# Summing the later modulations of a diffusion layer over partitions by block transposes and one 0/1 matrix, with fewer of their steps in the context's loop

## The chip, the core and the metric

The kernel runs on one core of a Trainium2 chip. Its time is the device time of one execution in microseconds, of which the median of several runs counts. The engines are named as in the profile: PE is TensorE's matmul side and PEld its weight loads, DVE is VectorE, ACT is ScalarE, POOL is GpSimd, SP is the engine whose queue issues nearly all transfers here.

## What is computed

One layer of a diffusion backbone over 1024 latent tokens and 256 context tokens of 1024 channels, all in float32: a gated feed-forward half step, a mixer (short convolution beside grouped-query attention), and a second half step. Each of the three parts is normalised and modulated by a shift, a scale and a gate, which are rows of one vector per stream (latent `l`, context `c`):

```python
mod_lat = (jax.nn.silu(c) @ w_mod[layer] + b_mod[layer])[:, None, :]
mod_ctx = (jax.nn.silu(c_ctx) @ w_mod[layer] + b_mod[layer])[None, None, :]
ml = jnp.split(mod_lat, N_MOD, axis=-1)          # nine rows of 1024
x = x + 0.5 * ml[2] * swiglu(modulate(rms_norm(x, norm1_g[layer]), ml[0], ml[1]), ...)
...
x = x + 0.5 * ml[8] * swiglu(modulate(rms_norm(x, norm3_g[layer]), ml[6], ml[7]), ...)
```

`w_mod` is 1024 by 9216. The latent stream needs all nine rows of it, the context stream the first five. In the kernel a modulation row is a table with the channel on the partition: channel 128j + p stands in column j of partition p.

## The kernel before, in words

**Products.** The large products run on PE as three fp32r matmuls of 128x128 by 128x512 each (high by high, high by low, low by high), and by a Winograd scheme, so that one "product" is 12 matmuls. Weights arrive by a load on SP's queue into a tile `raw`; POOL adds and subtracts them into tiles `s` where the scheme needs it; ACT casts them to fp32r and DVE subtracts the cast, which gives a pair called `wl` in the traces (`split`, L189). Four such pairs can wait ahead of PE (`W_BUFS`), five PSUM banks `ps` take products, two banks `pt` take short results and transposes, one bank `po` is left.

**Stages.** After a head (tokens are loaded, turned and normalised, the first modulations are made by another way, `column_mod` and `second_mod`) comes the first half step, L1337: a loop over 22 columns j of the hidden layer. For each j PE does five products (`second`, `third`), DVE and ACT finish the hidden columns, and SP stores them (`hd`). At j = 11 a second loop runs inside, the **context's loop** (L1347): for i = 0 to 11 the context's 256 tokens are multiplied with the weights of the columns already done, in matmuls of 256 columns (`h1ch`, `h1cl`), and every second i their hidden columns go through the second weight (`hidc`, `wo`, sums in `cacc`). From j = 12 on the context's products run along with the latent ones (`side`, L1262). Then come the half step's output (`row_products`, L1429), the mixer's products with the convolution (L1445 on), queries and keys, the attention, the merge, the second half step (its loop over 22 columns at L2158) and the last norm.

**Later modulations.** All modulation rows that are not needed in the head are made by the generator `later_mod` (L266), in halves of 512 channels. For each half it loads eight tiles `rawm` of `w_mod` (128x512, 256 KB each), and DVE adds each, times a column of silu(c), into an accumulator `macc` of 128x512 per stream. So 128 partial sums stand on the partitions for each of 512 channels. Then, per stream: ACT and DVE split `macc` into two fp32r tiles (`acch`, `accl`), PE multiplies a column of ones (`ones_r`, 128x1) with each (two matmuls with an output of 1x512 in a bank `pt`), ACT copies that row out (`mrow`), four small transfers on SP's queue lay the row out on 128 partitions (`mcol`), and DVE adds the bias into `modl` or `modc`. In all 22 streams are summed: one each for the context's second halves of rows 1 and 0, twelve for rows 2 to 4, two for row 5, four for rows 6 and 7, two for row 8.

**Who calls it.** The generator is advanced step by step: `run(steps, n)` takes n steps. In the first half step the number per j is `STEPS` (L43), and in the context's loop 3 per i (L1353). The steps of rows 1, 0, the context's norm (`normc`, which makes `h1ch` and `h1cl`) and rows 2 to 5 lie in `steps`; rows 6 and 7 are taken during the mixer's products (L1457, L1460), row 8 in the second half step (L2160).

**What sets the order.** Every instruction is recorded in the program's order and then placed by a scheduler, which works with a time line of its own and puts instructions of an engine where it expects them to be ready. The engines then run their lists strictly in order. Instructions recorded as pinned (`matmul(..., pinned=True)`, L132) keep the program's order among each other. Short tiles of 128x512 (`rawm`, `macc`, `s`, `u`, `c`, `v`, `b`, `nt` and others) share one pool of 11 buffers (L102, `ttile`), so that a tile of one kind can wait for the release of another kind.

**The norm of the second half step.** `norm1` of the class `Winograd` (L526) takes the sum of squares over channels, which lies on the partitions in two accumulators `sq_acc` and `sq`, and sums it by eight matmuls with `ones` as the moving operand (`rstd_cols`, L245), which puts token 128j + p on partition p of column j; an inverse root follows on DVE (`rs_a`, `rs_t`, `rs_y`), which is then spread by PE (`bcast`). The mixer's object is made with `plain=True`, that of the second half step is not; the first half step has its root from elsewhere.

Of the kernel before, what the change touches and what calls it, by code (L numbers as in the profile page):

```python
# [9 lines left out]
F32 = mybir.dt.float32  # L10
F32R = mybir.dt.float32r
I32 = mybir.dt.int32
AF = mybir.ActivationFunctionType
ALU = mybir.AluOpType
AX = mybir.AxisListType
# [3 lines left out]
P = 128  # L19
D = 1024  # L20
# [8 lines left out]
EPS = 1e-6  # L29
# [10 lines left out]
AHEAD = 3  # L40
FILLS = (24,) + 4 * (11,) + 11 * (10,)
SIDE_FROM = 12
STEPS = (0, 4, 4, 4, 4, 5, 5, 5, 5, 5, 5, 4, 11)  # L43
WAIT = 4
AH1, HALVES, WH = 12, 8, (4, 5, 6, 7, 12, 13, 14, 15, 20, 21, 22, 23)
RESIDENT, AH2, AH3 = 2, 9, 12
# [5 lines left out]
def tile_dit_layer(  # L52
# [63 lines left out]
    def ttile(name, n=512, dt=F32):  # L116
        t = tpool.tile([P, 512], dt, tag="t", name=uniq(name))
        return t[:, :n]

    def small(name, n, dt=F32):  # L120
        return spool.tile([P, n], dt, tag=f"s{n}_{name}", name=uniq(name))
# [4 lines left out]
    def ps_t(n=512):  # L126
        return psum.tile([P, 512], F32, tag="t", name=uniq("pt"), bufs=2)[:, :n]
# [4 lines left out]
    def matmul(out, w, x, start, stop, pinned=False, on=False):  # L132

        inst = pe.matmul(out, w, x, start=start, stop=stop, skip_group_check=on)
        if pinned or in_order[0]:
            tc.keep_in_program_order(inst)
# [14 lines left out]
    make_identity(nc, ident[:])  # L151
    ones = const.tile([P, 1], F32, name="ones")
    dve.memset(ones[:], 1.0)
    ones_r = const.tile([P, 1], F32R, name="ones_r")
    act.copy(out=ones_r[:], in_=ones[:])


    cols = const.tile([P, P], F32, name="cols")
# [30 lines left out]
    def split(src, hi, lo, lo_eng=None, hi_eng=None):  # L189

        if hi_eng is dve:
            dve.tensor_copy(out=hi, in_=src)
        else:
            act.copy(out=hi, in_=src)
        (lo_eng or dve).tensor_sub(out=lo, in0=src, in1=hi.bitcast(F32))
# [43 lines left out]
    def rsqrt_cols(a, n):  # L239

        y = small("rs_y", n)
        rsqrt_into(y[:], small("rs_t", n)[:], a)
        return y

    def rstd_cols(accs, n, dim):  # L245
# [10 lines left out]
        dve.tensor_scalar(out=a[:], in0=pss, scalar1=dim * EPS, scalar2=None, op0=ALU.add)  # L256
        return rsqrt_cols(a[:], nt)

    def bcast(y, n):

        pr = ps_t(n)
        for j in range(n // P):
            transpose(pr[:, j * P : (j + 1) * P], y[:, j : j + 1].to_broadcast([P, P]), pinned=True)
        return pr

    def later_mod(m, halves=(0, 1), streams=None):  # L266

        if streams is None:
            streams = (0, 1) if m < 5 else (0,)
        for half in halves:  # L270
            accs = [ttile(f"macc{v}") for v in streams]
            o = m * D + half * 512
            for k in range(KD):
                raw = ttile("rawm")
                load(out=raw, in_=w_mod[0, k * P : (k + 1) * P, o : o + 512])
                for acc, v in zip(accs, streams):
                    s = silu_c[:, v * 8 + k : v * 8 + k + 1]
                    if k == 0:
                        dve.tensor_scalar(out=acc, in0=raw, scalar1=s, scalar2=None, op0=ALU.mult)
                    else:  # L280
                        dve.scalar_tensor_tensor(out=acc, in0=raw, scalar=s, in1=acc, op0=ALU.mult, op1=ALU.add)
                yield
            for _ in range(WAIT):
                yield
            for acc, v in zip(accs, streams):
                ah, al = ttile("acch", dt=F32R), ttile("accl", dt=F32R)
                split(acc, ah, al)
                for _ in range(3):
                    yield
                mod, pm = (modl, modc)[v], ps_t()  # L290
                matmul(pm[:1], ones_r[:], ah, start=True, stop=False, pinned=True)
                matmul(pm[:1], ones_r[:], al, start=False, stop=True, pinned=True)
                row = ttile("mrow")
                act.copy(out=row[:1], in_=pm[:1])
                mcol = small("mcol", 4)
                for j in range(4):
                    sp.dma_start(out=mcol[:, j : j + 1], in_=row[:1, j * P : (j + 1) * P])
                c0 = m * 8 + half * 4
                dve.tensor_add(out=mod[:, c0 : c0 + 4], in0=mcol[:], in1=bcol[:, c0 : c0 + 4])
            yield  # L300

    def summed_mod(m, half, acc):
# [139 lines left out]
    def run(steps, n=None):  # L442

        if n is None:
            for _ in steps:
                pass
        else:
            for _ in range(n):
                next(steps, None)
# [13 lines left out]
    class Winograd:  # L463
# [60 lines left out]
            self.n_squares[ch] = n + 1  # L524

        def norm1(self):  # L526
            y = self.rstd1 or rstd_cols(self.accs[C1], 512, D)
            yield
            pr = bcast(y, 512)
            yield  # L530
            late = {3: [], 4: [], 7: []}
            for k in range(4):
                f, h, t34 = self.h0[k], atile("h12", (P, 2, 512)), atile("t34", (P, 2, 512))
                b12, b22, t3, t4 = h[:, 0], h[:, 1], t34[:, 0], t34[:, 1]
                for i, b in ((k, b12), (k + 4, b22)):
                    dve.tensor_mul(out=b, in0=self.xs(i, C1), in1=pr)
                    self.shifted(b, i)
                t1, t2 = ttile("nt"), ttile("nt")
                dve.tensor_sub(out=t1, in0=b12, in1=f[:, 0])
                dve.tensor_sub(out=t2, in0=b22, in1=t1)  # L540
                dve.tensor_sub(out=t4, in0=t2, in1=f[:, 1])
                self.keep(6, k, t2)
                dve.tensor_sub(out=t3, in0=b22, in1=b12)
                self.keep(5, k, t1)
                for i, t in ((3, b22), (4, t4), (7, t3)):
                    late[i].append(t)
                yield
            for i in (7, 4, 3):
                for k, t in enumerate(late[i]):
                    self.keep(i, k, t)  # L550
                yield
# [785 lines left out]
    for j in range(NH):  # L1337
        half1.side = side(j) if j >= SIDE_FROM else None
        if j > SIDE_FROM and j % 2:
            raws = context_rows(j)  # L1340
        u, c = half1.next_first()
        v, b = half1.second(u)
        spill(c, b, j, C0)
        spill(*half1.third(u, v), j, C1)
        run(steps, STEPS[min(j, len(STEPS) - 1)])
        if j == SIDE_FROM - 1:
            for i in range(SIDE_FROM):  # L1347
                if i % 2 == 0:
                    raws = context_rows(i + 1)
                do = side(i, ps_s)  # L1350
                for step in (1, 2, 0, 4):
                    do(step, half1.left())
                run(steps, 3)  # L1353
                if i % 2 == 0:
                    context_last()
                    ws = context_parts(i + 1, raws)
                else:
                    pending.append((i, ws))
        elif j > SIDE_FROM and j % 2:
            pending.append((j, context_parts(j, raws)))  # L1360
        elif j >= SIDE_FROM:
            context_last()
# [875 lines left out]
```

## Time and profile before

| | |
|---|---|
| median of 3 runs | 2657.49 us (2656.51 to 2659.11) |
| the profiled execution | 2662.96 us, of which its span is 2661.2 us |
| PE busy | 2609.7 us (98%), 13337 matmuls |
| DVE busy | 2054.2 us (77%) |
| ACT busy | 1229.3 us (46%) |
| POOL busy | 549.2 us (21%) |
| share of PE in the chain that ended last | 82% |

The share of the busy time tells which engine is full, not where it waits. Matmuls overlap, so that one of 391 ns in the table of groups costs PE less: what one costs is the distance from its start to the next one's. A time line's row gives start and duration, the operation, the tiles as out<-in, the shape of the stationary operand (rows*columns), the output's shape, the number of merged instructions, and in brackets the engine's idle time before it with what ended that. A row of windows gives, for each engine, busy time and number of instructions in that stretch, then the granted clock of PE (1.00 is full) and the share of the 16 DMA engines.

### The profile page before, as it was taken

The page shows a single profiled execution, that of the slowest core. Times are in us where ns is not written, and L with a number is a line of the kernel's source. Part 1 is how long each engine was busy: PE and PEld are TensorE (multiplying, and loading weights), DVE is VectorE, ACT ScalarE, POOL GpSimd, SP SyncE. Part 2 cuts the span into 40 slices and gives each one's busy share as a digit, 9 for nine tenths or more (in the row PEclk, how much of TensorE's full clock was granted, in tenths as well). Part 3 has the DMA queues.
Part 4 walks back from the last instruction along what each step waited for, and adds up shares of the span by engine and source line. Part 5 has one row for each costly group of instructions (what it writes and reads, how often), then busy time and mean ns, then how long its engine had stood idle before and what let it go on. Part 6 is the DMA issues. An engine that isn't in the chain of part 4 may idle for free.

```text
span 2661.2 us, 37166 instructions
## 1 busy us (share of the span) xinstructions
PE 2609.7 (98%) x13337; PEld 2197.8 (83%) x13337; DVE 2054.2 (77%) x3366; ACT 1229.3 (46%) x2434; POOL 549.2 (21%) x374
## 2 busy tenths in 40 slices
PE   8999999999999999999999999999999999999998
PEld 5788998888788878888898788788887888888888
DVE  5988887786887898887687766676888777666885
ACT  5633443333454643333366666666437333334444
POOL 1243011221010044332310011111030334320110
PEclk9999999999999999999999999999999999999999
DMA  8656753345984355443536321122443654327841
GB/s 269 223 183 192 230 171 119 112 127 195 314 187 108 106 170 171 132 141 113 172 123 207 103 64 64 60 68 64 133 126 123 202 179 135 98 76 258 224 100 68
DMA packets 386128, 393.14 MB, mean 148 GB/s; under 512 B 29326, under 2 KB 268056, under 8 KB 385944
## 3 DMA queue, kind: packets, MB, share of 16 engines
q1 hardware_dynamic: 376920, 373.48, 43.8%
q0 software_dynamic: 9024, 17.30, 4.0%
q8 instruction: 104, 1.70, 0.3%
q14 instruction: 80, 0.66, 0.1%
HBM read 313.07 MB, written 77.59 MB: 147 GB/s over the span
## 4 chain that ended last, share of the span: by engine, by line
PE 82%; DVE 8%; DMA 4%; ACT 3%; issue 2%; SPq 1%; POOL 1%; DVEq 0%; ACTq 0%; POOLq 0%
PE ps L90 67%; PE po L90 7%; PE pt L90 7%; DVE wl L90 1%; ACT pl L90 1%; DVE pts L90 1%; DVE u L90 1%; DMA rawm<-in_w_mod_dram 1%; DMA o<-qd 1%; DMA hid<-hd 1%; SPq L90 1%; DVE r L90 1%; DMA y<-yd 1%; DVE v L90 1%; DVE m L90 1%
## 5 line engine op out<-in xcount | busy, mean ns | idle before, releaser
L90 PE MATMUL ps<-r,wl 128*128 128x512 f32 x5496 | 1272.7, 391 | 14.2 <-DVE wl L90 6.2
L90 PEld LDWEIGHTS ps<-r,wl 128*128 128x128 f32 x5496 | 1030.4, 189 | 234.3 <-DVE wl L90 8.7
L90 ACT CAST wl<-s 128x512 fp32r<-128x512 f32 x266 | 164.2, 619 | 339.6 <-PE ps L90 254.3
L90 ACT CAST wl<-raw 128x512 fp32r<-128x512 f32 x298 | 184.0, 620 | 230.8 <-PE ps L90 124.7
L90 DVE TENSOR_TENSOR wl<-raw,wl 128x512 fp32r<-128x512 f32 x296 | 213.9, 728 | 74.9 <-ACT wl L90 74.0
L90 POOL TENSOR_TENSOR s<-raw 128x512 f32<-128x512 f32 x68 | 98.9, 1454 | 819.2 <-DMA raw<-in_ffn_w_in_dram 369.9
L90 DVE TENSOR_TENSOR wl<-s,wl 128x512 fp32r<-128x512 f32 x266 | 235.4, 886 | 32.6 <-ACT wl L90 31.1
L90 POOL TENSOR_TENSOR s<-raw,s 128x512 f32<-128x512 f32 x68 | 103.6, 1524 | 363.5 <-DVE wl L90 354.4
L90 DVE SCALAR_TENSOR_TENSOR macc<-rawm,silu_c,macc 128x512 f32<-128x512 f32 x168 | 147.9, 893 | 11.8 <-DMA rawm<-in_w_mod_dram 11.2
L90 DVE TENSOR_REDUCE m<-ps 128x1 f32<-128x512 f32 (+1 forms) x192 | 110.8, 595 | 59.4 <-PE ps L90 59.4
L90 DVE TENSOR_TENSOR u<-u,ps 128x512 f32<-128x512 f32 x183 | 124.1, 678 | 27.2 <-PE ps L90 26.8
L90 ACT CAST pts<-pt 128x512 fp32r<-128x512 f32 x160 | 93.8, 587 | 102.3 <-PE pt L90 102.2
L90 PE MATMUL ps<-tw,r 128*128 128x256 f32 x1008 | 126.6, 287 | 5.7 <-DVE tw L90 5.3
L90 PEld LDWEIGHTS ps<-tw,r 128*128 128x128 f32 x1008 | 123.7, 194 | 6.6 <-DVE tw L90 5.9
L90 DVE TENSOR_TENSOR pts<-pt,pts 128x512 fp32r<-128x512 f32 x160 | 109.4, 685 | 24.1 <-ACT pts L90 21.7
L90 PE MATMUL ps<-rh,wl 128*128 128x512 f32 x360 | 122.2, 390 | 0.0
L90 ACT CAST rh<-hid 128x512 fp32r<-128x512 f32 x132 | 80.8, 619 | 85.1 <-PE ps L90 76.6
L90 PE MATMUL po<-pts,v 128*128 128x512 f32 x384 | 120.1, 422 | 0.0
L90 ACT ACTIVATE pl<-ps,nm,qscale 128x512 f32<-128x512 f32 x128 | 98.6, 775 | 42.8 <-DVE nm L90 42.7
L90 POOL TENSOR_TENSOR s<-raw,raw 128x512 f32<-128x512 f32 x74 | 112.0, 1513 | 9.6 <-DVE macc L90 3.3
L90 PE MATMUL ps<-kl,qs 128*128 128x512 f32 x384 | 110.2, 395 | 2.5 <-ACT pl L90 2.2
L90 PE MATMUL ps<-y,wc 128*128 128x512 f32 x384 | 105.5, 395 | 1.9 <-DVE g L90 1.9
(361 smaller groups left out, 4648.1 us busy)
## 6 DMA issues: line engine op xcount, KB each, us to landing
raw<-in_ffn_w_in_dram SPq DMA_DIRECT2D x128, 512.0 KB
raw<-in_ffn_w_out_dram SPq DMA_DIRECT2D x72, 512.0 KB
rawm<-in_w_mod_dram SPq DMA_DIRECT2D x128, 256.0 KB
raw<-in_w_in_dram SPq DMA_DIRECT2D x53, 512.0 KB
hid<-hd SPq DMA_DIRECT2D x40, 512.0 KB
ws<-in_ffn_w_out_dram POOLq DMA_DIRECT2D x30, 512.0 KB, 6.3
ucd<-uc SPq DMA_DIRECT2D x26, 512.0 KB
hd<-c SPq DMA_DIRECT2D x39, 256.0 KB
```

What stands on the lines that cost most here:

```text
L90: inst = getattr(self.engine, name)(*args, **kw)
```

## The change

`later_mod` sums over partitions in another way. For each stream DVE transposes `macc` in blocks of 32x32 (`mturn`), so that a block's 32 partial sums of one channel lie in one row, and adds them up with one reduction over 32 neighbours; 16 numbers per partition are left, which are written over the start of the first accumulator. One float32 matmul per half, with the 0/1 matrix `same4` as the stationary operand (128x128, a one wherever row and column agree modulo 32), adds the four groups of 32 partitions and leaves the result on all four of them. DVE then takes from each group of 32 partitions the columns that belong to it: four additions of 32x4 per stream, which read PSUM and add the bias. The split, the matmuls with `ones_r`, the row's copy and the four transfers are gone. `same4` is made at the start by one reduction and one copy on DVE in place of a cast on ACT. The waits between steps are laid out so that a half still has as many steps.

`rstd_spread` does the same for the root in `norm1` where the object is not `plain`, which is the second half step alone.

Of the steps, those in the context's loop fall from 3 to 2 for i = 0 to 9 and to none for i = 10 and 11; `STEPS` falls by one for j = 5 to 11 and rises from 11 to 13 for j = 12 and later.

```diff
-STEPS = (0, 4, 4, 4, 4, 5, 5, 5, 5, 5, 5, 4, 11)
+STEPS = (0, 4, 4, 4, 4, 4, 4, 4, 4, 4, 4, 3, 13)
...
-    ones_r = const.tile([P, 1], F32R, name="ones_r")
-    act.copy(out=ones_r[:], in_=ones[:])
+    same = ttile("same", 32)
+    dve.reduce_sum(out=same, in_=ident[:].rearrange("p (g i) -> p i g", i=32), axis=AX.X)
+    same4 = const.tile([P, P], F32, name="same4")
+    dve.tensor_copy(out=same4[:].rearrange("p (g i) -> p g i", i=32), in_=same[:, None, :].to_broadcast([P, 4, 32]))
...
+    def rstd_spread(accs, n, dim):
+        nt = n // P
+        pss = ps_t(4 * nt)
+        for i, acc in enumerate(accs):
+            turned = ttile("sturn", n)
+            dve.transpose(out=turned, in_=acc)
+            red = acc[:, : 4 * nt]
+            dve.reduce_sum(out=red, in_=turned.rearrange("p (b r) -> p b r", r=32), axis=AX.X)
+            matmul(pss, same4[:], red, start=(i == 0), stop=(i == len(accs) - 1), pinned=True)
...
-            for acc, v in zip(accs, streams):
-                ah, al = ttile("acch", dt=F32R), ttile("accl", dt=F32R)
-                split(acc, ah, al)
-                for _ in range(3):
-                    yield
-                mod, pm = (modl, modc)[v], ps_t()
-                matmul(pm[:1], ones_r[:], ah, start=True, stop=False, pinned=True)
-                matmul(pm[:1], ones_r[:], al, start=False, stop=True, pinned=True)
-                row = ttile("mrow")
-                act.copy(out=row[:1], in_=pm[:1])
-                mcol = small("mcol", 4)
-                for j in range(4):
-                    sp.dma_start(out=mcol[:, j : j + 1], in_=row[:1, j * P : (j + 1) * P])
-                c0 = m * 8 + half * 4
-                dve.tensor_add(out=mod[:, c0 : c0 + 4], in0=mcol[:], in1=bcol[:, c0 : c0 + 4])
+            n = len(streams)
+            red = accs[0][:, : 16 * n]
+            for i, acc in enumerate(accs):
+                turned = ttile("mturn")
+                dve.transpose(out=turned, in_=acc)
+                dve.reduce_sum(
+                    out=red[:, 16 * i : 16 * i + 16], in_=turned.rearrange("p (b r) -> p b r", r=32), axis=AX.X
+                )
+                yield
+                yield
+            pm = ps_t(16 * n)
+            matmul(pm, same4[:], red, start=True, stop=True, pinned=True)
+            c0 = m * 8 + half * 4
+            for i, v in enumerate(streams):
+                for g in range(4):
+                    rows = slice(32 * g, 32 * g + 32)
+                    dve.tensor_add(
+                        out=(modl, modc)[v][rows, c0 : c0 + 4],
+                        in0=pm[rows].rearrange("p (v j g) -> p v j g", v=n, g=4)[:, i, :, g],
+                        in1=bcol[rows, c0 : c0 + 4],
+                    )
+                yield
             yield
...
-            y = self.rstd1 or rstd_cols(self.accs[C1], 512, D)
+            y = self.rstd1 or (rstd_cols if self.plain else rstd_spread)(self.accs[C1], 512, D)
...
-                run(steps, 3)
+                run(steps, 2 if i < SIDE_FROM - 2 else 0)
```

Three places show how the scheduler's lists move. The first is DVE's list at the end of the context's loop, before: `macc` and `rawm` belong to a later modulation, `wo` and `cacc` to the context's output, and the two `wl` at the end are parts of the first weights after the loop.

```order
L90 SCALAR_TENSOR_TENSOR macc_651_3654<-rawm_3739,silu_c,macc_651_3654 128x512
L90 SCALAR_TENSOR_TENSOR macc_652_3655<-rawm_3739,silu_c,macc_652_3655 128x512
L90 TENSOR_TENSOR cacc_1105<-cacc_1105,ps_3779 128x512
L90 TENSOR_TENSOR cacc_1105<-cacc_1105,ps_3793 128x512
L90 TENSOR_TENSOR wo_3813<-raw_3666,wo_3813 128x512
L90 SCALAR_TENSOR_TENSOR macc_651_3654<-rawm_3743,silu_c,macc_651_3654 128x512
L90 TENSOR_TENSOR wo_3816<-raw_3666,wo_3816 128x512
L90 SCALAR_TENSOR_TENSOR macc_652_3655<-rawm_3743,silu_c,macc_652_3655 128x512
L90 TENSOR_TENSOR wl_3845<-raw_3835,wl_3845 128x512
L90 TENSOR_TENSOR wl_3860<-raw_3835,wl_3860 128x512
```

And the same place of DVE's list with the change, up to the same two `wl`:

```order
L90 TENSOR_TENSOR cacc_1106<-cacc_1106,ps_3659 128x512
L90 TENSOR_TENSOR cacc_1106<-cacc_1106,ps_3673 128x512
L90 TENSOR_TENSOR wo_3715<-raw_3584,wo_3715 128x512
L90 TENSOR_TENSOR hidc_3653<-sa_3654,hidc_3653 128x256
L90 TENSOR_TENSOR cacc_1107<-cacc_1107,ps_3687 128x512
L90 TENSOR_TENSOR wo_3718<-raw_3584,wo_3718 128x512
L90 TENSOR_TENSOR cacc_1107<-cacc_1107,ps_3701 128x512
L90 TENSOR_TENSOR wo_3721<-raw_3586,wo_3721 128x512
L90 TENSOR_TENSOR wo_3724<-raw_3586,wo_3724 128x512
L90 TENSOR_TENSOR wl_3753<-raw_3743,wl_3753 128x512
L90 TENSOR_TENSOR wl_3768<-raw_3743,wl_3768 128x512
```

The four instructions of the later modulation that stood ahead of the two `wl` are gone from there. The second place is SP's queue at the same point; `raw` from `in_ffn_w_in` are the weights, `raw_3835` and `raw_3837` before and `raw_3743` and `raw_3745` after the first ones behind the loop. Before:

```order
L90 DMA raw_3686<-in_ffn_w_in_dram 128x8x128
L90 DMA rawm_3656<-in_w_mod_dram 128x512
L90 DMA mcol_3648<-mrow_3646 128x1x1 x4
L90 DMA rawm_3660<-in_w_mod_dram 128x512
L90 DMA raw_3835<-in_ffn_w_in_dram 128x8x128
L90 DMA raw_3837<-in_ffn_w_in_dram 128x8x128
L90 DMA rawm_3739<-in_w_mod_dram 128x512
L90 DMA rawm_3743<-in_w_mod_dram 128x512
```

With the change:

```order
L90 DMA raw_3606<-in_ffn_w_in_dram 128x8x128
L90 DMA rawm_3576<-in_w_mod_dram 128x512
L90 DMA rawm_3580<-in_w_mod_dram 128x512
L90 DMA raw_3743<-in_ffn_w_in_dram 128x8x128
L90 DMA raw_3745<-in_ffn_w_in_dram 128x8x128
L90 DMA raw_3916<-in_ffn_w_in_dram 128x8x128
L90 DMA raw_3918<-in_ffn_w_in_dram 128x8x128
```

The four transfers `mcol` have left the queue, and behind the two weights come the next two weights where loads of `w_mod` stood. The third place is PE's list at the first sum of the half step's loop (the context's second half of row 1). Before, the two matmuls with the column of ones stand among the products:

```order
L90 MATMUL pt_1668<-acch_1664,ones_r 1x512
L90 MATMUL ps_1688<-r_132_654,wl_1606 128x512 x2
L90 MATMUL ps_1706<-r_175_878,wl_1626 128x512 x2
L90 MATMUL ps_1688<-r_132_654,wl_1606 128x512
L90 MATMUL ps_1688<-r_138_702,wl_1606 128x512 x2
L90 MATMUL pt_1668<-accl_1665,ones_r 1x512
L90 MATMUL ps_1688<-r_138_702,wl_1606 128x512
```

With the change one matmul stands there, with 16 columns:

```order
L90 MATMUL ps_1684<-r_133_656,wl_1608 128x512 x2
L90 MATMUL ps_1702<-r_176_880,wl_1628 128x512 x2
L90 MATMUL ps_1684<-r_133_656,wl_1608 128x512
L90 MATMUL ps_1684<-r_139_704,wl_1608 128x512 x3
L90 MATMUL ps_1684<-r_150_761,wl_1608 128x512 x2
L90 MATMUL pt_1669<-macc_261_1318,same_84 128x16
L90 MATMUL ps_1684<-r_150_761,wl_1608 128x512
```

Two rows of 512 columns have become one of 16, at nearly the same point among the products.

More of the change, by code (lines that the diff above doesn't have):

```diff
@@ L257, in rstd_cols @@
         return rsqrt_cols(a[:], nt)
+    def rstd_spread(accs, n, dim):
[7 more added lines that the diff above has]
+            matmul(pss, same4[:], red, start=(i == 0), stop=(i == len(accs) - 1), pinned=True)
+        a = small("rs_a", nt)
+        for g in range(4):
+            rows = slice(32 * g, 32 * g + 32)
+            dve.tensor_scalar(
+                out=a[rows], in0=pss[rows].rearrange("p (j g) -> p j g", g=4)[:, :, g], scalar1=dim * EPS,
+                scalar2=None, op0=ALU.add,
+            )
+        return rsqrt_cols(a[:], nt)
     def bcast(y, n):
@@ L284, in later_mod @@
                 yield
-            for acc, v in zip(accs, streams):
-                ah, al = ttile("acch", dt=F32R), ttile("accl", dt=F32R)
-                split(acc, ah, al)
-                for _ in range(3):
-                    yield
-                mod, pm = (modl, modc)[v], ps_t()
-                matmul(pm[:1], ones_r[:], ah, start=True, stop=False, pinned=True)
-                matmul(pm[:1], ones_r[:], al, start=False, stop=True, pinned=True)
-                row = ttile("mrow")
-                act.copy(out=row[:1], in_=pm[:1])
-                mcol = small("mcol", 4)
-                for j in range(4):
-                    sp.dma_start(out=mcol[:, j : j + 1], in_=row[:1, j * P : (j + 1) * P])
-                c0 = m * 8 + half * 4
-                dve.tensor_add(out=mod[:, c0 : c0 + 4], in0=mcol[:], in1=bcol[:, c0 : c0 + 4])
+            n = len(streams)
[12 more added lines that the diff above has]
+            for i, v in enumerate(streams):
+                for g in range(4):
+                    rows = slice(32 * g, 32 * g + 32)
+                    dve.tensor_add(
+                        out=(modl, modc)[v][rows, c0 : c0 + 4],
+                        in0=pm[rows].rearrange("p (v j g) -> p v j g", v=n, g=4)[:, i, :, g],
+                        in1=bcol[rows, c0 : c0 + 4],
+                    )
+                yield
             yield
```

## The prediction

> **What bounds the kernel now.** First the page's span and busy times, then the windows of a quiet stretch.
>
> ```profile
> span 2661.2 us, 37166 instructions
> PE 2609.7 (98%) x13337; PEld 2197.8 (83%) x13337; DVE 2054.2 (77%) x3366; ACT 1229.3 (46%) x2434; POOL 549.2 (21%) x374
> ```
>
> ```profile
> core 0: us, PE busy (x) PEld busy (x) DVE busy (x) ACT busy (x) POOL busy (x), PEclk, DMA share, GB/s
> 1100.00:1150.00 50.00, 50.00 (x222) 41.07 (x221) 42.44 (x64) 15.46 (x27) 15.30 (x11) 1.00 0.37 108
> ```
>
> PE is busy for 98%, but a busy share alone could hide slack, because a matmul of 128x512 is drawn with 0.39 us and overlaps the next. The count settles it: 222 matmuls in 50 us are one per 0.225 us, at the full granted clock and without a gap. A PE-bound stretch therefore gets shorter by the distance that each removed matmul takes in the row, and by each wait of PE that goes; work that leaves ACT, SP or DVE counts only where PE waits for it. Next I looked where PE waits near the change, in the time line and the chain that ended last. Two waits of the first half step have to do with the later modulations. The first, in the chain of waits, lies at the end of the context's loop:
>
> ```profile
> 371.21 2.05 DMA mcol<-mrow
> ...
> 374.89 7.00 DMA rawm<-in_w_mod_dram
> ...
> 382.46 1.78 DVE macc L90
> ```
>
> ```profile
> 388.62 4.15 PE L90 MATMUL ps<-r,wl 128*128 128x512 f32 x10 [2.35 <-DVE wl L90]
> ```
>
> SP's queue waits for the small transfers `mcol`, issues `rawm` late, DVE stands at `macc` until it lands, and the `wl` that PE needs is behind that `macc` in DVE's list. The second is earlier, at the last columns ahead of that loop (PE, then POOL, then DVE):
>
> ```profile
> 269.03 0.73 PE L90 MATMUL ps<-r,wl 128*128 128x512 f32 x2 [2.12 <-ACT wl L90]
> 270.17 6.19 PE L90 MATMUL ps<-r,wl 128*128 128x512 f32 x20 [0.40 <-DVE wl L90]
> ```
>
> ```profile
> 263.77 3.21 POOL L90 TENSOR_TENSOR s<-raw 128x512 f32<-128x512 f32 x1 [9.66 <-DVE macc L90]
> ```
>
> ```profile
> 262.83 0.87 DVE L90 TENSOR_SCALAR macc<-rawm,silu_c 128x512 f32<-128x512 f32 x2
> ```
>
> POOL had to wait 9.66 us for a buffer of the shared pool, until `macc` had read `rawm`; its sums `s` came late, then ACT's cast and DVE's `wl`. Both waits cost more than their gap, since the clock granted to PE falls behind them:
>
> ```profile
> 260.00:280.00 20.00, 17.47 (x70) 13.62 (x69) 17.91 (x31) 7.82 (x15) 7.38 (x4) 0.91 0.69 208
> 300.00:320.00 20.00, 20.00 (x168) 19.77 (x166) 12.18 (x23) 12.37 (x25) 0.00 (x0) 1.00 0.87 242
> 380.00:400.00 20.00, 17.65 (x100) 15.37 (x100) 18.84 (x26) 5.74 (x10) 10.05 (x7) 0.91 0.34 99
> ```
>
> **The change part by part.** *PE, sums.* The stretch around the last sum before, with the two matmuls of a stream, and their groups (count, busy time and mean, idle time before them):
>
> ```profile
> 2239.70 2.88 PE L90 MATMUL ps<-r,wl 128*128 128x512 f32 x12
> 2242.41 0.40 PE L90 MATMUL pt<-acch,ones_r 128*1 128x512 f32 x1
> 2242.65 0.40 PE L90 MATMUL pt<-accl,ones_r 128*1 128x512 f32 x1
> 2242.88 2.46 PE L90 MATMUL ps<-r,wl 128*128 128x512 f32 x10
> ```
>
> ```profile
> L90 PE MATMUL pt<-acch,ones_r 128*1 128x512 f32 x22 | 8.7, 396 | 0.0
> L90 PE MATMUL pt<-accl,ones_r 128*1 128x512 f32 x22 | 8.7, 396 | 0.0
> ```
>
> From 2242.41 to 2242.88 the pair takes 0.47 us of the row although it has only one column of weights: 22 pairs are 10.3 us, all on the path. In their place come 16 float32 matmuls, one per half, of 16 or 32 columns. The nearest rows are the float32 sums of the second half step's norm, eight matmuls that leave 16 records:
>
> ```profile
> 2024.68 0.28 PE L90 MATMUL pt<-ones,sq_acc 128*128 128x1 f32 x2
> ...
> 2026.16 0.36 PE L90 MATMUL pt<-ones,sq 128*128 128x1 f32 x2
> 2026.39 7.33 PE L90 MATMUL ps<-r,wl 128*128 128x512 f32 x31
> 2033.56 0.60 PE L90 MATMUL pt<-ident,rs_y 128*128 128x128 f32 x4
> 2033.91 0.48 PE L90 MATMUL ps<-r,wl 128*128 128x512 f32 x1
> ```
>
> 16 records in 1.71 us are 0.107 each, with one column; the four transposes of 128 columns take 0.35 us, 0.088 each; a full 512 columns take 0.225. So the 32 new records cost between 2.8 and 7.2 us; I take 0.107, as 16 columns are nearest to one: 3.4 us. *PE, norm.* Those 16 records become 4, which gives 1.71 - 0.43 = 1.3 us. PE alone: -10.3 + 3.4 - 1.3 = **-8.2 us**.
>
> *DVE.* Prices, as distances from start to start, from the end of the context's loop and from the root of that norm, and the groups:
>
> ```profile
> 386.62 0.68 DVE L90 TENSOR_TENSOR wo<-raw,wo 128x512 fp32r<-128x512 f32 x1
> 387.22 0.74 DVE L90 SCALAR_TENSOR_TENSOR macc<-rawm,silu_c,macc 128x512 f32<-128x512 f32 x1
> 387.88 1.28 DVE L90 TENSOR_TENSOR wl<-raw,wl 128x512 fp32r<-128x512 f32 x2
> ```
>
> ```profile
> 2027.32 0.16 DVE L90 TENSOR_TENSOR rs_t<-rs_t,rs_a 128x4 f32<-128x4 f32 x1
> 2027.52 0.16 DVE L90 SCALAR_TENSOR_TENSOR rs_y<-rs_t,rs_y 128x4 f32<-128x4 f32 x1
> ...
> 2028.70 0.16 DVE L90 SCALAR_TENSOR_TENSOR rs_y<-rs_t,rs_y 128x4 f32<-128x4 f32 x1
> ```
>
> ```profile
> L90 DVE SCALAR_TENSOR_TENSOR macc<-rawm,silu_c,macc 128x512 f32<-128x512 f32 x168 | 147.9, 893 | 11.8 <-DMA rawm<-in_w_mod_dram 11.2
> L90 DVE TENSOR_REDUCE m<-ps 128x1 f32<-128x512 f32 x128 | 87.9, 687 | 59.4 <-PE ps L90 59.4
> ```
>
> Per stream a subtraction (0.60) and one small addition (0.20) go. A block transpose is nowhere in the trace; its nearest rows over 512 elements lie between 0.4 us (the pair of scalings in 0.87 above) and 0.89 (the mean of `macc`, waits for ports included); I take 0.60, the pace of a plain pass. The reduction is like `m`: 0.69 drawn, as long as the subtraction, so 0.60. Four small additions are 0.80. That is 2.0 in place of 0.8 us, 1.2 more per stream, 26 us for 22 streams (22 to 39 by those bounds). The Trainium skill (Vector Engine (DVE) Microarchitecture Reference, section 3.8, The reshape front-end and per-opcode configuration) says that the 32x32 transpose sustains one element per cycle per lane, which is the pace of a plain pass; by it the 26 us stand, and no row of before shows it.
>
> Whether this shows depends on the stretch. 23 of the steps also move behind the context's loop (50 + 36 up to there before, 43 + 20 after), and a step holds 8/19 of two `macc` of 0.66 us: 13 us. Where they go, there is room:
>
> ```profile
> 388.00:675.00 287.00, 286.38 (x1595) 249.60 (x1596) 219.61 (x333) 96.02 (x172) 54.30 (x37) 0.99 0.44 141
> 1000.00:1100.00 100.00, 100.00 (x443) 82.81 (x442) 89.11 (x131) 33.33 (x59) 39.07 (x26) 1.00 0.54 168
> ```
>
> DVE's 219.6 us there become 219.6 + 13 + 11 streams (half of row 2, rows 3 and 4, one of row 5) x 1.2 = 246 of 287, 86%; in the mixer DVE stands at 89% with PE gapless. PE's cover is the up to four `wl` made ahead, four products of 2.7 us; where it is gone, a wait costs its gap and the clock, about 4 us as below. In-order lists add two new waits: PE stands at a sum until both reductions are done, with the next products behind it, and DVE stands at the small additions until PE has done the sum, with the next `wl` behind them. For these I take **+2 us** (0 to 4).
>
> *SP, ACT.* The transfers and DVE's wait for them:
>
> ```profile
> L90 SPq DMA_DIRECT2D mcol<-mrow x88: 470/594/1663, 186.8 to 2246.1; - x88
> ```
>
> 88 issues of 0.59 us, 52 us of SP's queue, go, and each had stood in front of weight loads until ACT's row was out. ACT's casts and copies go too; ACT is off the path. In the first wait the order with the change has neither `mcol` ahead of `rawm` nor `macc` ahead of the two `wl`, and the two weight loads stand earlier in SP's queue. I count it as gone. Its price: 2.35 us of gap, and the ten matmuls behind it took 4.15 us where ten at full pace take 2.88 - 2 x 0.225 = 2.43: **-4.1 us**. What is next ahead of those two `wl` are four `cacc` and `wo` of 0.6 us each, which need only products that PE has done by then. For the second wait: 2.12 + 0.40 us of gap, and 20 matmuls took 6.19 where 2.88 + 8 x 0.225 = 4.68 are due, 4.0 in all. There the scaling that POOL waited for has moved behind these columns, but the context's norm and `wo` crowd the same columns and the pool still has 11 buffers: I take half, **-2.0 us** (0 to -4.0).
>
> *Norm chain.* Two transposes, two reductions, three more small additions: 3.0 us later on DVE, 1.3 earlier from PE. Before, the root is done at 2028.86 and PE turns it at 2033.56; the 4.7 us between cover it. If they did not, PE would lose up to 1.7 us. *Head.* The two instructions for `same4` fall into DVE's idle start:
>
> ```profile
> 3.32 0.18 DVE L90 COPY cols<-pt 128x24 f32<-128x24 f32 x1 [2.44 <-PE pt L90]
> ```
>
> *Sum.* -8.2 - 4.1 - 2.0 + 2.0 = -12.3 us against the profiled execution's 2662.96, which gives 2650.7. The median of the runs without a profile is 2657.49, 5.5 lower, and I carry the difference over: **2645.2 us**. Differences within 0.2%, 5.3 us, count as the same, about what a measurement can tell.
>
> **The rivals.** *A, PE's work alone.* The two waits stay or turn up a few products later, because DVE's list around them is as full as before; for it speaks that DVE gains work in these very stages. 2657.5 - 8.2 = 2649.3. *B, the gain is half given back.* The old waits stay and one more of 4.1 us appears where 13 steps per column meet the context's `wo`: 2653.4. *C, PE has slack.* If the loading of weights were PE's measure, its 83% would leave 17% free and removed matmuls would buy nothing: 2657.5. Against it, 222 matmuls in 50 us leave no room. The Trainium skill (Perfetto Trace Analysis, section Identifying the Most-Contended Engine) calls matmul busy time a poor measure and wants weight loads judged instead; the trace agrees that 0.39 us per matmul overlaps, but its pace contradicts the slack. *D, slower: DVE's reductions stop PE.* A sum's matmul stands in PE's list at a fixed place; if DVE reaches its transposes later than the scheduler thought, PE stops there, with the clock falling behind. It decides when DVE's lead over PE at a sum is under the 2.4 us of two transposes and two reductions. With all of DVE's 26 us uncovered: 2657.5 + 26.4 - 8.2 = 2675.7. For it speaks the 9.66 us wait above, against it that the 44 matmuls of before, which depended on DVE in the same way, had no idle time ahead of them (the 0.0 of their groups).
>
> **How the numbers follow.** Forecast 0.54, A 0.18, B 0.14, C 0.04, D 0.07, and 0.03 for more than the forecast. The forecast's own range is 2641.2 (second wait gone, nothing new) to 2649.3 (it stays, and 4 new). Reaching over A and B, with 2 us for the price of the new matmuls at the low side, the range is 2639 to 2654; C, D and the outer part of B are left out. Faster: 0.54 + 0.18 + 0.03 = 0.75; same: 0.14 + 0.04 = 0.18; slower: 0.07.
>
> **What would show it.** Right: `macc`, `same4` in 32 records about 0.11 apart with no gap of PE ahead of them; no gap over 1 us between 380 and 390 us, and the granted clock at 1.00 there; DVE near 85% from there to the output product; block transposes near 0.68 us drawn. Wrong: gaps of PE that end with DVE `macc`, or new gaps ending with `wl` in columns 12 to 21; or a time unchanged although the 44 matmuls are gone.

## The result, and the profile after

The changed kernel takes 2642.6 us (median of 4 runs, 2641.06 to 2643.59) where the kernel before, run beside it, takes 2657.0: a ratio of 0.9944, 95% interval 0.9932 to 0.9957. That is 14.4 us less; 12.3 less was forecast, 2645.2 us. Its profiled execution is 2642.17 us. The first rows of its page:

```profile
span 2640.4 us, 36969 instructions
PE 2593.3 (98%) x13313; PEld 2189.6 (83%) x13313; DVE 2072.1 (78%) x3463; ACT 1207.4 (46%) x2388; POOL 545.1 (21%) x374
```

The two profiled executions differ by 20.8 us, more than the medians. A second profiled execution of the kernel before (2658.25 us, below) is 4.7 us shorter than the first, so that much of the 20.8 is one long execution. Differences between kernels are therefore taken from medians here, and the traces are read for where something waits.

The windows of the two waits, and of the stretch behind the context's loop (columns as before):

```profile
260.00:280.00 20.00, 20.00 (x95) 16.74 (x94) 19.97 (x37) 9.54 (x18) 3.46 (x3) 1.00 0.60 171
300.00:320.00 20.00, 19.37 (x162) 19.17 (x161) 17.11 (x31) 13.25 (x27) 0.00 (x0) 1.00 0.68 204
380.00:400.00 20.00, 20.00 (x112) 17.41 (x111) 10.62 (x16) 5.60 (x10) 4.18 (x4) 1.00 0.40 124
388.00:675.00 287.00, 286.56 (x1616) 251.45 (x1615) 242.98 (x414) 89.46 (x158) 47.91 (x34) 1.00 0.52 168
```

Both waits are gone, with the granted clock at 1.00 where it was 0.91. DVE is busy for 243.0 of 287 us behind the loop; 246 had been worked out. Between 380 and 400 us it fell from 18.84 us to 10.62. The new operations, by tile (count, shortest, median and longest duration in ns):

```profile
L90 PE MATMUL pt<-macc,same x32: 177/227/275, 185.1 to 2222.0; 128*128 128x16 f32 x20, 128*128 128x32 f32 x12
L90 DVE STREAM_TRANSPOSE mturn<-macc x22: 659/704/711, 178.2 to 2204.4; 128x512 f32<-128x512 f32 x22
L90 DVE TENSOR_REDUCE macc<-mturn x22: 661/672/683, 180.0 to 2206.6; 128x16 f32<-128x512 f32 x22
```

The last sum in PE's row, and its transpose in DVE's:

```profile
2206.75 15.36 PE L90 MATMUL ps<-r,wl 128*128 128x512 f32 x67
2221.94 0.29 PE L90 MATMUL pt<-macc,same 128*128 128x16 f32 x2
2222.08 6.16 PE L90 MATMUL ps<-r,wl 128*128 128x512 f32 x26
```

```profile
2204.42 0.70 DVE L90 STREAM_TRANSPOSE mturn<-macc 128x512 f32<-128x512 f32 x1
2205.05 1.02 DVE L90 TENSOR_TENSOR wl<-s,wl 128x512 fp32r<-128x512 f32 x1
```

PE has no gap ahead of the sum, and from 2221.94 to 2222.08 it takes 0.14 us of the row, where the forecast had 0.21 (two records of 0.107). The transpose takes 0.63 us to the next start, against 0.60 assumed, the pace of a plain pass. The trace so agrees with the sentence of the Trainium skill that the prediction cited (Vector Engine (DVE) Microarchitecture Reference, section 3.8).

What PE still waits for longest behind the context's loop, in the first half step, is the start of its output product, two gaps:

```profile
695.52 0.50 PE L90 MATMUL pt<-rh,wl 128*128 128x512 f32 x1 [1.52 <-ACT wl L90]
699.20 0.73 PE L90 MATMUL pt<-rh,wl 128*128 128x512 f32 x2 [1.58 <-DVE wl L90]
```

### The profile page after: what moved, and what is told of

The parts are those of the page before. It is cut to its first block, busy times and chain, and to the rows that moved or that the text cites. A ratio compares the mean times of both kernels' runs of the same rounds, so it can differ in the third digit from the quotient of the medians.

```text
span 2640.4 us, 36969 instructions
## 1 busy us (share of the span) xinstructions
PE 2593.3 (98%) x13313; PEld 2189.6 (83%) x13313; DVE 2072.1 (78%) x3463; ACT 1207.4 (46%) x2388; POOL 545.1 (21%) x374
## 4 chain that ended last, share of the span: by engine, by line
PE 84%; DVE 8%; ACT 4%; DMA 2%; issue 2%; POOL 0%; SPq 0%; DVEq 0%; POOLq 0%; ACTq 0%
PE ps L90 70%; PE po L90 8%; PE pt L90 7%; ACT pl L90 1%; DVE pts L90 1%; DVE r L90 1%; DMA raw<-in_ffn_w_in_dram 1%; DVE wl L90 1%; DVE m L90 1%; ACT r L90 0%; ACT pts L90 0%; ACT wl L90 0%; DVE v L90 0%; DVE u L90 0%; DMA xtok<-in_ctx_dram 0%
## 5 line engine op out<-in xcount | busy, mean ns | idle before, releaser
L90 DVE SCALAR_TENSOR_TENSOR macc<-rawm,silu_c,macc 128x512 f32<-128x512 f32 x168 | 141.8, 860 | 8.5 <-DMA rawm<-in_w_mod_dram 8.0
```

Source lines behind the costliest of these rows:

```text
L90: inst = getattr(self.engine, name)(*args, **kw)
```

## The experiments

The theory behind the forecast: PE's row gets shorter by the matmuls that go, DVE's added work lies beside PE, and the two waits go because the transfers `mcol` no longer delay `rawm` and `macc`, and because steps have moved. The first half step is the stretch in which the steps move; its end, with the output product, comes up again and again below. The change has three parts, called sums, table (`STEPS`) and loop (`run` in the context's loop). All comparisons by parts in one table (us; the kernel before had medians of 2656.7 to 2657.8 beside them):

| sums | table | loop | median | ratio, 95% interval |
|---|---|---|---|---|
| new | new | new | 2642.6 | 0.9944 (0.9932 to 0.9957), the change |
| new | old | old | 2650.5 | 0.9975 (0.9966 to 0.9984) |
| old | new | new | 2656.6 | 0.9996 (0.9986 to 1.0006) |
| old | new | old | 2649.5 | 0.9974 (0.9966 to 0.9983) |
| new | new | old | 2641.2 | 0.9938 (0.9924 to 0.9951) |
| new | old | new | 2653.2 | 0.9981 (0.9972 to 0.9990) |
| new | old, 13 late | new | 2643.2 | 0.9955 (0.9941 to 0.9968) |

Of the eight ways to join the parts, the old sums and the old table with the new loop were not run.

### The sums alone, the steps alone

The first two experiments split the change: the changed kernel with the old steps, and the old kernel with the new ones.

```diff
-STEPS = (0, 4, 4, 4, 4, 4, 4, 4, 4, 4, 4, 3, 13)
+STEPS = (0, 4, 4, 4, 4, 5, 5, 5, 5, 5, 5, 4, 11)
...
-                run(steps, 2 if i < SIDE_FROM - 2 else 0)
+                run(steps, 3)
```

> The new sums with the steps where they were before (3 per i in the context's loop, the old table per column). Theory: PE's work alone is worth about 9.3 us (22 pairs of 0.47 us gone, 16 sums of about 0.14 us come, 1.2 us in the norm), and this kernel has all of it; of the waits at the end of the context's loop it keeps the one on rawm, without the transfers mcol ahead of it, so that a gap of 0 to 2 us with its 1.7 us of lower clock may stay. Time 2645 to 2648 where before is 2657.0 and the change 2642.6. Rival, the moved steps are the whole gain: as before, 2656 to 2658, with both gaps (2.5 and 2.35 us). Rival, the transfers mcol made the waits: as the change, 2642 to 2644, with no gap over 1 us between 260 and 400 us.

Measured 2650.48 us, a gain of 6.2: less than expected and outside its range, a miss. Both waits are still there, although no `mcol` is left in the program. PE's rows, and the window at the loop's end:

```profile
267.90 0.73 PE L90 MATMUL ps<-r,wl 128*128 128x512 f32 x2 [0.91 <-ACT wl L90]
269.59 4.67 PE L90 MATMUL ps<-r,wl 128*128 128x512 f32 x19 [0.96 <-DVE wl L90]
```

```profile
385.39 3.39 PE L90 MATMUL ps<-r,wl 128*128 128x512 f32 x10 [2.32 <-DVE wl L90]
```

```profile
380.00:400.00 20.00, 17.68 (x92) 15.14 (x91) 20.00 (x28) 5.47 (x10) 6.40 (x4) 0.91 0.18 54
```

DVE is busy for 20.00 of 20 us: at the loop's end PE waits for a DVE that is full. So `mcol` is not what makes this wait; that part of the prediction's chain is refuted. The rest of it stands: in the chain that ended last here, a `rawm` still lands at 371.86 us, and from then on the chain runs on DVE, with pauses of at most 1.02 us, through `macc`, `cacc` and `wo` to the `wl` at 384.66 for which PE waits. The reverse edit, the old kernel with the new table and the new loop:

> The old sums (two matmuls with a column of ones, a row's copy, four transfers) with the new step table and fewer steps in the context's loop. Theory: both waits of PE in the first half step hang on where macc and rawm stand in the lists of DVE and SP, so they go although mcol stays; PE's work stays. 2657.0 less 4 to 8 us: 2649 to 2653, and 44 matmuls of 1x512 still 0.235 us apart. Rival, mcol makes the waits: 2656 to 2658, gaps of 2 us still there. Rival, the steps are the whole gain of 14 us: 2642 to 2645.

Measured 2656.56 us: no gain at all, a miss. Neither wait is left in its trace; what took the gain back stands at the start of the output product. PE's row, and ACT's just ahead of it:

```profile
707.15 0.80 PE L90 MATMUL pt<-rh,wl 128*128 128x512 f32 x1 [5.58 <-ACT wl L90]
```

```profile
706.48 0.62 ACT L90 CAST wl<-raw 128x512 fp32r<-128x512 f32 x1 [4.48 <-DMA raw<-in_ffn_w_out_dram]
```

PE waits for ACT, ACT for a transfer that lands late. This is rival B's "half given back", at another place than B named, and the whole gain instead of half.

### PE's work put back

Two idle matmuls of 1x512 per stream, `ones_r` with itself, are put ahead of each new sum, 44 in all. Their result is not used.

```diff
+            for _ in range(2 * n):
+                matmul(idle[:1], ones_r[:], ones_r[:].to_broadcast([P, 512]), start=True, stop=True, pinned=True)
             matmul(pm, same4[:], red, start=True, stop=True, pinned=True)
```

> The change, with PE's removed work put back by itself: ahead of each sum stand two matmuls of 1x512 per stream that multiply a constant and are read by nobody, 44 in all. DVE, ACT and SP do what they do in the change. Theory, PE is the bound and each costs its distance in the row, 0.235 us: 2642.6 + 10.3 = 2652.9, between 2651 and 2655. Rival C, PE has slack that its busy share hides: 2642 to 2644.

Measured 2651.46 us, ratio 0.9983 (0.9974 to 0.9992): 8.9 us more than the change, 0.20 per matmul, where their pace in the row is 0.235. Their group:

```profile
L90 PE MATMUL pt<-ones_r 128*1 128x512 f32 x44 | 12.2, 380 | 0.0
```

So matmuls off the products' path cost nearly their place in the row: rival C, that PE has slack, falls. The weight loads' 83%, by which the Trainium skill (Perfetto Trace Analysis, section Identifying the Most-Contended Engine) would judge the headroom, says nothing of it here. (That section names it beside the share of peak work that the products reach, which was not worked out here.)

### DVE's work made larger

Each stream gets two more block transposes, which cancel each other: 44, or some 28 us of DVE at 0.63.

```diff
                 dve.transpose(out=turned, in_=acc)
+                dve.transpose(out=acc, in_=turned)
+                dve.transpose(out=turned, in_=acc)
```

> The change, with two more block transposes of 128x512 per stream on DVE in each sum (there and back, the result is the same): 44 passes of about 0.6 us, 26 us more of DVE's work, as much again as the change added, and 1.2 us later per stream at the sum. Theory, DVE's work lies beside PE's: at most 3 us longer, 2642 to 2646. Rival D, PE stands at the sums until DVE is done: 16 sums that wait 1.2 to 2.4 us each and then run at a lower clock, 20 us or more, 2662 and up.

Measured 2643.55 us, ratio 0.9953 (0.9941 to 0.9966), not to be told from the change. The stretch behind the loop takes the work in, and PE's idle time there stays under half a microsecond:

```profile
388.00:675.00 287.00, 286.65 (x1617) 251.81 (x1617) 254.17 (x438) 89.04 (x157) 48.35 (x34) 1.00 0.50 165
```

DVE rises by 11.2 us there, PE stays at 286.65. Rival D, that DVE's reductions stop PE, falls.

### The kernel before once more

> The kernel before, profiled a second time, to see which of its waits are fixed and which are chance. Theory: the waits ahead of and at the end of the context's loop (about 2.1 and 2.4 us, near 267 and 386 us) are there again, since they come from the order of the lists; the 4.0 us near 1302 us shrinks to under 2.5, as it did in the first two variants, and the span is 2652 to 2658. Rival: the two waits vary as freely as the third, and then no variant can be judged by them.

```profile
268.33 5.98 PE L90 MATMUL ps<-r,wl 128*128 128x512 f32 x17 [2.12 <-ACT wl L90]
```

```profile
387.28 2.58 PE L90 MATMUL ps<-r,wl 128*128 128x512 f32 x10 [1.06 <-DVE wl L90]
```

One execution: 2658.25 us, span 2656.5. The gap ahead of the loop is the same to 0.01 us (2.12), without the second one of 0.40 behind it. The one at the loop's end is less than half as long as in the first profile, so half of what was expected fails: this wait does vary. Its price of 4.1 us was read from the longer of two executions, and small differences between the gaps of two traces are not read below.

### Whose queue takes the gain back

A first guess was that with the old sums the last `mcol` issues stand in SP's queue ahead of the output product's loads. Here the old sums with the new steps issue them on ACT.

```diff
-                    sp.dma_start(out=mcol[:, j : j + 1], in_=row[:1, j * P : (j + 1) * P])
+                    act.dma_start(out=mcol[:, j : j + 1], in_=row[:1, j * P : (j + 1) * P])
```

> Old sums, new step table and loop, and the four small transfers mcol of each sum issued by ACT behind its copy of the row, not by SP. Theory S: moving the steps alone gave nothing because the last sums of the half step then put their mcol issues into SP's queue ahead of the loads of the output product (a gap of 5.75 us there against 2.13 before); with SP free of them the gap falls under 2.5 us and the time to 2653 (2651 to 2655). Rival V: DVE's own steps, crowded behind the loop, make that product late; the gap stays over 4 us and the time at 2656 to 2658.

```profile
704.33 0.79 PE L90 MATMUL pt<-rh,wl 128*128 128x512 f32 x1 [5.38 <-ACT wl L90]
```

Measured 2657.38 us, ratio 0.9996 (0.9987 to 1.0005), and the gap stays: the guess falls. Two edits apart, with the new sums, tell where the steps matter:

> New sums, new step table, the context's loop with its old 3 steps a turn. Theory: the table relieves the columns ahead of the loop, so the wait near 267 us goes and the one at the loop's end (2.3 us of gap, 4.1 with the clock) stays: the change's 2642.6 + 4.1 = 2646.7 (2645 to 2648.5). Rival: the loop's turns alone make both waits, and the table does nothing: 2650.5 as with both old.

> New sums, old step table, the context's loop with the new 2 steps a turn and none at the end. Theory: the wait at the loop's end goes and the one ahead of it stays (2.7 us of gaps, 4.0 with the clock): 2642.6 + 4.0 = 2646.6 (2645 to 2648.5). Rival: the loop alone is the whole effect: 2642.6 (2641 to 2644).

The table alone gives 2641.19 us, the whole gain; the loop alone gives 2653.17, no better than with neither (0.9981 against 0.9975, with intervals that overlap). Both theories missed, each in its own way. The wait at the loop's end has gone in both runs, as DVE is relieved there by either edit. It is busy for 9.33 of 20 us with the loop alone, and for 13.05 with the table alone:

```profile
380.00:400.00 20.00, 20.00 (x110) 17.43 (x111) 13.05 (x22) 6.02 (x11) 5.57 (x4) 1.00 0.37 119
```

The wait ahead of the loop goes with the table and stays with the loop alone:

```profile
267.07 0.73 PE L90 MATMUL ps<-r,wl 128*128 128x512 f32 x2 [0.94 <-ACT wl L90]
268.76 5.50 PE L90 MATMUL ps<-r,wl 128*128 128x512 f32 x16 [0.95 <-DVE wl L90]
```

With the loop alone the last half of a row comes too late. By the code there are 32 steps for rows 1 and 0, 8 for the context's norm, 114 for rows 2 to 4 and 32 for row 5, 186 in all. By the end of the last column 50 + 20 + 110 = 180 of them are taken, so six are left (not 17, as an expectation further down has it). But the last half's eight loads fall to the last column itself, and its sum comes behind it. The loads are issued at the end of the half step, and PE stops there (SP's rows, then PE's):

```profile
660.11 0.33 SPq L90 DMA_DIRECT2D rawm<-in_w_mod_dram  x1
...
664.20 3.29 SPq L90 DMA_DIRECT2D rawm<-in_w_mod_dram  x7
```

```profile
676.13 2.07 PE L90 MATMUL ps<-rh,wl 128*128 128x512 f32 x4 [6.22 <-ACT rh L90]
```

### Transfers at the end of the half step

This suggested another theory: the end of the half step, where `hid`, `x` and the output weights are loaded, is limited by transfers. In the changed kernel, and in the old sums with the new steps:

```profile
650.00:670.00 20.00, 19.57 (x109) 16.68 (x108) 16.75 (x33) 7.63 (x14) 0.00 (x0) 1.00 1.02 363
670.00:690.00 20.00, 20.00 (x96) 16.78 (x95) 16.13 (x22) 7.69 (x13) 1.36 (x1) 1.00 1.06 366
```

```profile
650.00:670.00 20.00, 19.44 (x109) 16.71 (x108) 12.51 (x21) 7.04 (x14) 0.00 (x0) 1.00 1.05 387
690.00:710.00 20.00, 14.42 (x59) 11.51 (x58) 16.59 (x22) 7.08 (x12) 2.59 (x2) 0.87 1.07 346
```

The last two columns show the DMA engines full. By the theory this stretch starts with the first load of `hid` on SP's queue, and the output product can begin when its transfers are through. Before (SP, then PE):

```profile
645.87 10.98 SPq L90 DMA_DIRECT2D hid<-hd  x13
```

```profile
709.60 0.50 PE L90 MATMUL pt<-rh,wl 128*128 128x512 f32 x1 [1.97 <-ACT wl L90]
```

That is 63.7 us. With the change, `hid` starts here, and the product at 695.52, 63.4 us later; two `rawm` loads were issued 4 us ahead of the stretch, five more 9.6 us ahead (at 622.57):

```profile
628.22 0.99 SPq L90 DMA_DIRECT2D rawm<-in_w_mod_dram  x2
...
632.17 11.62 SPq L90 DMA_DIRECT2D hid<-hd  x13
```

With the old sums and the new steps seven `rawm` loads stand directly in front, and 64.9 us pass to 707.15:

```profile
638.77 3.38 SPq L90 DMA_DIRECT2D rawm<-in_w_mod_dram  x7
642.25 12.83 SPq L90 DMA_DIRECT2D hid<-hd  x13
```

With the loop alone eight `rawm` loads stood inside the stretch, and it took 73.1 us (from 635.95 to 709.06). The chain that ended last bears the theory out for the old sums with the new steps: it runs over transfers of `rawm`, `hid`, `x` and `raw` there (in the kernel before over `hid` and `raw`). In the changed kernel it runs over PE's products and then DVE, so there the transfers are full but are not shown to be the limit.

So, by the theory, steps moved behind the loop gain only if they are done ahead of that stretch. The old sums with the table alone, which takes 16 more steps in the loop, test this:

> Old sums, new step table, the context's loop with its old 3 steps a turn, so that the last sum of the half step is done some 30 us ahead of its end. Theory T (transfers at the boundary): from 640 to 710 us the DMA engines are full (share 1.05, 385 to 390 GB/s), the output product starts 63 to 66 us after the first load of hid, and moving the steps alone gave nothing because seven rawm loads then stood ahead of hid and in that full stretch; with them done early the gap there is under 3 us, both waits of PE are gone, and the time is 2649 (2647 to 2651). Rival: the old sums with their transfers hold the gain back wherever they stand: 2655 to 2657.

```profile
612.13 1.00 SPq L90 DMA_DIRECT2D rawm<-in_w_mod_dram  x1
639.90 11.95 SPq L90 DMA_DIRECT2D hid<-hd  x13
```

```profile
703.18 0.39 PE L90 MATMUL pt<-rh,wl 128*128 128x512 f32 x1
...
706.10 0.73 PE L90 MATMUL pt<-rh,wl 128*128 128x512 f32 x2 [0.94 <-DVE wl L90]
```

Measured 2649.49 us, as the theory had it: the old sums gain 7.8 us by the table alone (2657.26 beside them), and what is left of the gap is 0.94. But the product begins at 703.18 without a wait, 63.3 us after `hid`: here PE's own work fills the same distance, which therefore doesn't tell by itself whether transfers or PE set it. The opposite test keeps the loop's edit and the old table ahead of it, but gives 13 steps in place of 11 to each column from j = 12 on, so that the last loads come at least a column earlier and no step is left over:

```diff
-STEPS = (0, 4, 4, 4, 4, 4, 4, 4, 4, 4, 4, 3, 13)
+STEPS = (0, 4, 4, 4, 4, 5, 5, 5, 5, 5, 5, 4, 13)
```

> New sums, the context's loop as changed, the table old ahead of the loop but 13 steps a column behind it in place of 11, so that no step is left at the end of the half step (17 were left in the run with the loop alone, at 2653.2). Theory T: no rawm load in the full stretch, the gap of 6.4 us at the boundary shrinks to under 2; the wait ahead of the loop, 2.7 us of gaps, stays: 2641.2 + 4 = 2645.2 (2644 to 2648). Rival: the loop's edit costs by itself, 2651 to 2654.

Median 2643.24 us, a little below the expected range, with runs up to 2647.08. The stop of 6.2 us is gone, one of 2.25 us is left at the product, and the wait ahead of the loop stays:

```profile
267.39 0.73 PE L90 MATMUL ps<-r,wl 128*128 128x512 f32 x2 [0.91 <-ACT wl L90]
269.08 5.12 PE L90 MATMUL ps<-r,wl 128*128 128x512 f32 x21 [0.95 <-DVE wl L90]
...
701.77 0.73 PE L90 MATMUL pt<-rh,wl 128*128 128x512 f32 x2 [2.25 <-DVE wl L90]
```

The rival is refuted. What the earlier wait costs the interval can't tell: by the medians it is 0.6 us more than the change, by the ratios 2.9, and 4 had been expected.

### The norm's part, and more of the same

> The change without its part on the norm (16 one-column float32 records in place of 4, two transposes and two reductions less on DVE). Theory: PE's 1.3 us come back, 2643.9 (2643 to 2645.5). Rival: the norm's longer chain on DVE had eaten the gain: 2642.6 or less.

The edit puts `rstd_cols` back in `norm1`. Measured 2642.26 us, ratio 0.9946 (0.9934 to 0.9959): no difference from the change, where 1.3 us more were expected, as the rival had it. In the changed kernel PE waits once behind that norm; with the old norm the same stretch is one row without a gap:

```profile
2058.76 3.51 PE L90 MATMUL ps<-r,wl 128*128 128x512 f32 x14 [0.34 <-DVE wl L90]
```

```profile
2049.80 12.40 PE L90 MATMUL ps<-r,wl 128*128 128x512 f32 x54
```

That gap is 0.34 us and can't eat 1.3. The traces give a finer measure than the medians: from the gap of 0.68 us ahead of this norm to that of 0.67 us ahead of the last norm, the changed kernel takes 634.60 us (1996.70 to 2631.30), with the old norm 635.54 (1995.91 to 2631.45). Five more variants with the new norm lie between 634.5 and 635.1. So the norm's part does save something like 0.5 to 1 us, too little for the medians.

Since the table alone was the fastest variant, one more run took it further: `rstd_spread` in the mixer's norm and in `norm0` too.

> New sums, new table, old loop (2641.2 alone), and the two other norms of the first half step and the mixer also summed by transposes. Theory: 1.3 us of PE's row less for each norm: 2638.6 (2637.5 to 2640). Rival: there the root is waited for, and the 3.0 us that DVE's chain gets longer show instead: 2641 to 2647.

Measured 2651.07 us, 9.9 more than without, and worse than the rival had it. At `norm0` of the second half step PE stands until DVE has transposed and reduced:

```profile
1974.95 0.58 PE L90 MATMUL pt<-sq_acc,same 128*128 128x16 f32 x2 [2.72 <-DVE sq_acc L90]
1976.29 0.58 PE L90 MATMUL pt<-sq,same 128*128 128x16 f32 x2 [0.76 <-DVE sq L90]
```

Behind a norm of the mixer two gaps end with DVE, where the change has only one, of 0.84 us, that ends with ACT:

```profile
877.76 0.50 PE L90 MATMUL ps<-r,wl 128*128 128x512 f32 x1 [1.72 <-DVE x L90]
880.28 7.89 PE L90 MATMUL ps<-r,wl 128*128 128x512 f32 x22 [2.02 <-DVE r L90]
```

The stop at the sum is the mechanism of rival D, where DVE has no lead; how the 9.9 us divide between the two places was not taken apart. The change itself is not beaten: the table alone (0.9924 to 0.9951) can't be told from it (0.9932 to 0.9957), and drops an edit.

## Why the prediction held, point by point

- **PE's work, -8.2 us.** The mechanism is right, three sizes were off. 16 sums at 0.14 us are 2.2 us, not 3.4; the 44 matmuls cost 8.9 us when put back, not 10.3; the norm is worth 0.5 to 1 us, not 1.3. The sums alone gave 6.2 us with the old steps, 8.3 with the new table.
- **DVE beside PE.** Right: 243 us against 246, and 44 further transposes cost nothing that can be told. (Of the bounds of 22 to 39 us for DVE's added work, the lower moves the transpose alone and the upper the reduction too; nothing hangs on them.)
- **First wait, -4.1 us, "`mcol` ahead of `rawm`".** It went, but this step of the reasoning failed: with no `mcol` left and the old steps it was still 2.32 us long, with DVE full, and with `mcol` kept and the new steps it was gone. Fewer steps in front, by the table or by the loop, took it away; that `macc` stands ahead of the `wl` in DVE's list was the half of the reasoning that held. Its price was read from the longer of two executions.
- **Second wait, half of 4.0.** It went whole, by the table alone. The table, with which both waits go, is worth 7.8 us with the old sums (2657.26 - 2649.49) and 9.3 with the new (2650.48 - 2641.19), not 6.1; with the new sums the wait at the product shrinks with it too (2.25 to 0.91 us), so the two waits' own price stays open.
- **New waits, +2.0.** None at the sums of the modulations; one of 0.63 us is new in the context's loop (at 302.59 us, DVE `sa`). The prediction looked for them inside the columns; the risk lay at the end of the half step, which it did not mention. With the new sums the loop's edit costs 1.4 us (2642.6 against 2641.2), less than can be told; with the old ones it cost 7.1.
- **Sum.** -12.3 forecast, -14.4 measured. PE's work was worth 6.2 to 8.3 us, not 8.2; the table 7.8 to 9.3, not 6.1 for the waits; the loop's edit cost 1.4 (less than can be told), where 2.0 had been set aside for new waits. That the total came so close is in part luck: these errors partly cancel, and the forecast has the larger of the two waits go in part for a reason that does not hold.

Open: with old and new sums the same number of steps stands in the same columns, yet with the old ones all seven of the last `rawm` loads come 3.5 us in front of `hid`, where with the new ones five of them come 9.6 us in front. The old sum's longer chain over ACT, transfers and DVE is the likely reason, but no run took it apart. That the full DMA engines set the product's start is argued, from the shares, from the chain of the old sums with the new steps and from the 73 us with eight loads more in the stretch; the 62.5 to 65.7 us of the other variants speak for it only where PE waits at the product, and no run took those transfers away. At the changed kernel's end of the half step it is the `wl` pairs that end the gaps, so a shorter stretch of transfers may not be all that is needed there.

## What to carry to other kernels

Read a wait's cause from whether the engine that it names was busy: a full engine wants fewer instructions in front, an idle one leads further back. Work that is moved out of a crowded stretch can have a deadline, here the next stretch that is full of transfers; look there for the gain if it does not arrive, and ask in which column the last loads now stand. A sum that moves from PE to DVE paid here where DVE has a lead on PE, and cost where PE stands waiting for that very number, as at `norm0` of the second half step.

## What had not been expected of the hardware

- A float32 matmul with 16 columns, two records in the trace, took 0.14 us of PE's row, less than the 0.23 of a single fp32r one of 512 columns.
- The transfers ran at 387 GB/s for 20 us. The Trainium skill (DMA: Bandwidth & Descriptors, section Where 436 GB/s comes from) names about 358 as the limit of one core, half of its memory's rate; the rows of this run on one core are above that.
- Behind a gap of 5.58 us the granted clock was 0.87 in a window of 20 us of which only the last 2.9 us lie behind the gap, behind one of 2.32 us 0.91 in a window with 14.6 us behind it.
- One and the same wait of the kernel before was 2.35 us in one execution and 1.06 in another, and the kernel's 27 runs in one job spread from 2653.1 to 2666.5 us, those of the changed kernel from 2641.1 to 2643.6 (4 runs).
